# Context modulation after the first products instead of inside them, in a one-core hybrid attention and HGRN2 layer

## The chip, the cores and the metric

The kernel runs on one core of one Trainium2 chip. The number that counts is device time in microseconds (us) for one execution; three timed runs of the kernel before gave a median of 2031.61 us (2031.46 to 2032.01). Engines are named as in the profile: PE (TensorE matmul), PEld (its weight loads), DVE (VectorE), ACT (ScalarE), POOL (GpSimd) and SP (SyncE, whose queue here issues every DMA).

## What is computed

One layer takes 2048 latent tokens `x` and 256 context tokens `ctx`, all of width 1024. What matters for the change is its beginning:

```python
mod = silu(c) @ w_ada + b_ada            # for the latent tokens
shift, scale, gate = split(mod, 3)
mod_c = silu(c_ctx) @ w_ada + b_ada      # for the context tokens, same weights
shift_c, scale_c, _ = split(mod_c, 3)
h_lat = x * (1 + scale) + shift
h_ctx = ctx * (1 + scale_c) + shift_c
p_lat, p_ctx = h_lat @ w_in, h_ctx @ w_in   # 18 column units of 256
```

The columns of the products feed two mixers, a differential attention (`aq`, `ak`, `av`, gate `ag`) and a two-way gated scan (`ff`, `fb` forget gates, `hi` values, `hq` queries, gate `hg`). Of the context only `ak`, `av`, `ff`, `fb` and `hi` are needed. Then come the mixers, one output projection with `gate`, and a layer norm.

## The kernel before

**Products.** A unit is 256 columns of `w_in`. Every product is made of three matmuls on split operands: weights and tokens are each split into a rounded part and a rest (`wh`, `wl`; `hh`, `hl`), and `wl*hh`, `wh*hl`, `wh*hh` are added up in PSUM. `project_cols` (L507) makes 128x512 tiles, `project_tokens` (L526) 128x256 tiles for `hi` and `av`. Tokens come in four blocks of 512 (0 to 3) and the context block (number 4, of 256).

**Startup.** `startup()` makes the products of `ff0` and `ff1` on blocks 0 and 1 in four steps of two k rows each (L329, 48 matmuls a step, 192 in all), while the modulation that they need is still being made. A step loads four 512 KB rows of `w_ada` (tiles `wsh`, two of shift and two of scale), two `x` tiles (`xst`) and 256 KB of each unit's weights (`hh`, `hl` as raw tiles). Four dot products on DVE (`row_dot`, L392) turn rows of `w_ada` into columns of `mod`; ACT applies them to `x` (L444 and L445, both 128x512), and DVE makes the rests `hl` (L448) and `wl` (L457).

**Context modulation.** In the same steps `context_modulation` makes the context's columns of `mod` from the same `wsh` tiles: a multiplication on POOL (L403, 128x1024, two operands), a sum on ACT (L404) and a bias on POOL (L405), 16 times. Its row `silu(c_ctx)` is spread over the partitions by four small matmuls into `pa` (L385).

**After startup.** `project(HG_UNITS[2:], [0, 1, NBLK])` makes the pairs `fb`, `hi`, `hq` on blocks 0, 1 and the context. `merge` runs `gate_row` beside it, which loads the eight `wgate` rows, reduces them on DVE and stores `gate_d` in 4-byte elements. Then `project_rest` runs `ff` on the context and all `HG_UNITS` on blocks 2 and 3, now with the scan (`hgrn`) merged in at one scan step for three yields. A unit's weights are loaded into one raw buffer (`wraw`), then split into one of two sets (`wp[i % 2]`), which is free when the unit two places back has no product left. A tile of `ff` or `fb` is evacuated by ACT twice and DVE twice (L562 to L566) and stored to `FD` and `KD`; one of `hq` by ACT and DVE once and stored to `HQ`. The evacuation tiles (`e1`, `e2`) have two buffers, each free again when its store has landed; PSUM has four tiles (`pd`) for these products.

**What sets the order.** Each engine and the SP queue works in a fixed order, which the compiler's scheduler chose from the program text; a DMA behind one that waits, waits too.

## Time and profile before

| | before |
|---|---|
| median of 3 runs | 2031.61 us |
| the profiled execution | 2032.69 us |
| its span, first to last instruction | 2030.9 us |
| PE busy | 1913.6 us (94%) |
| DVE, ACT, POOL busy | 71%, 45%, 47% |
| DMA mean | 137 GB/s |

The span is what the rows below divide; 1.8 us of the profiled execution lie outside it. A busy PE says little by itself, since matmuls are pipelined: the distance between the starts of two matmuls tells more. 128x512 matmuls of this kernel start 0.227 us apart at their fastest. Shares over the whole span hide that the stages have different limits, so the rows below are taken from the first 300 us.

### The profile page before, as it was taken

The numbers are of one execution on the slowest core, as the hardware profiler recorded it, in microseconds if no ns is written. First come the engines' busy times: TensorE is split into PE (matmuls) and PEld (weight loads), VectorE is DVE, ScalarE is ACT, GpSimd is POOL, SyncE is SP. The second block draws the span as 40 slices with busy tenths as digits, with TensorE's granted clock in tenths as the row PEclk, the third lists the DMA queues.
The fourth block names the chain that finished last, engine by engine and source line by source line (L and its number), as shares of the span: only waits on it lengthen the run. The fifth ranks groups of instructions, "written<-read, shape, count | busy, mean of one in ns | idle before, by whom it ended". The sixth has DMA issues, their size and how long they took to land.

```text
span 2030.9 us, 32106 instructions
## 1 busy us (share of the span) xinstructions
PE 1913.6 (94%) x11716; PEld 1693.3 (83%) x11716; DVE 1438.3 (71%) x3022; ACT 920.4 (45%) x1383; POOL 955.6 (47%) x697
## 2 busy tenths in 40 slices
PE   5899999999989999999879999999999999998887
PEld 3689888998878898877667999999999999887676
DVE  8940475455676755678454279999999999967878
ACT  6731233222222222232100168999998889852211
POOL 6400063343554532535110047877877767755543
PEclk8999999999989999999889999999999999999999
DMA  5772564523344543353657652261261031145442
GB/s 221 248 221 81 186 220 164 182 99 125 113 136 150 167 151 138 110 169 102 199 169 229 199 148 59 68 169 54 62 169 57 28 102 37 51 136 173 154 139 92
DMA packets 177760, 278.05 MB, mean 137 GB/s; under 512 B 16577, under 2 KB 108993, under 8 KB 175554
## 3 DMA queue, kind: packets, MB, share of 16 engines
q1 hardware_dynamic: 177602, 276.00, 42.6%
q8 instruction: 93, 1.52, 0.3%
q14 instruction: 65, 0.53, 0.1%
HBM read 178.94 MB, written 97.00 MB: 136 GB/s over the span
## 4 chain that ended last, share of the span: by engine, by line
PE 66%; DVE 14%; DMA 10%; issue 4%; POOL 3%; ACT 2%; SPq 1%; DVEq 0%; POOLq 0%; ACTq 0%
PE pd L507 18%; PE po L1089 9%; PE pd L526 9%; PE s L1002 6%; PE s L1003 6%; PE pt L1069 6%; PE pl L723 4%; PE py L1301 2%; DVE wl L457 2%; DMA QLd<-e 1%; DMA KLd<-e 1%; PE pm L755 1%; DVE y L1305 1%; DVE wh L456 1%; DVE qq L731 1%
## 5 line engine op out<-in xcount | busy, mean ns | idle before, releaser
L1017 DVE TENSOR_SCALAR_CACHE_REDUCE e<-s 128x512 f32<-128x512 f32 (+1 forms) x512 | 372.8, 751 | 31.9 <-PE s L1003 31.5
L507 PE MATMUL pd<-hh,wl 128*128 128x512 f32 (+1 forms) x928 | 371.8, 401 | 0.0
L507 PE MATMUL pd<-hl,wh 128*128 128x512 f32 (+1 forms) x928 | 355.6, 383 | 0.0
L507 PE MATMUL pd<-hh,wh 128*128 128x512 f32 (+1 forms) x928 | 355.5, 383 | 0.0
L1052 POOL TENSOR_TENSOR e<-e,e 128x768 f32<-128x768 f32 (+1 forms) x192 | 351.5, 1860 | 2.6 <-ACT e L1045 0.2
L1026 ACT ACTIVATE e<-e,nm 128x2304 f32<-128x2304 f32 x128 | 286.5, 2238 | 1.7 <-DVE nm L1021 1.5
L728 POOL TENSOR_TENSOR kk<-kk,fb 128x512 f32<-128x512 f32 x126 | 170.5, 1353 | 169.7 <-DMA kk<-KD 136.5
L1002 PE MATMUL s<-kh,q 128*128 128x512 f32 (+1 forms) x640 | 244.3, 388 | 1.2 <-DVE w1l L1076 0.6
L1003 PE MATMUL s<-kl,q 128*128 128x512 f32 (+1 forms) x640 | 231.4, 371 | 0.0
L507 PEld LDWEIGHTS pd<-hh,wh 128*128 128x128 f32 x928 | 177.0, 191 | 34.3
L507 PEld LDWEIGHTS pd<-hh,wl 128*128 128x128 f32 x928 | 177.9, 192 | 27.6 <-DVE wl L457 0.5
L507 PEld LDWEIGHTS pd<-hl,wh 128*128 128x128 f32 x928 | 177.8, 192 | 27.1
L718 ACT COPY km<-kk 128x512 f32<-128x512 f32 x112 | 71.0, 635 | 271.6 <-POOL kk L728 179.9
L1047 POOL TENSOR_SCALAR e<-e,cf 128x1280 f32<-128x1280 f32 x64 | 86.2, 1346 | 175.3 <-DVE cf L1037 121.3
L1069 PE MATMUL pt<-eye,e 128*128 128x128 f32 x1152 | 162.8, 272 | 2.4 <-DVE rs L1268 0.9
L734 POOL TENSOR_TENSOR fb<-fb 128x512 f32<-128x512 f32 (+6 forms) x126 | 88.3, 701 | 162.4 <-DVE qq L731 152.3
L526 PE MATMUL pd<-wh,hl 128*128 128x256 f32 x512 | 150.8, 295 | 4.1 <-ACT wh L456 4.1
L723 PE MATMUL pl<-qq,km 128*128 128x128 f32 x896 | 131.3, 291 | 24.7 <-DVE qq L731 23.0
L723 PEld LDWEIGHTS pl<-qq,km 128*128 128x128 f32 x896 | 122.9, 197 | 37.1 <-issue 25.4
L1069 PEld LDWEIGHTS pt<-eye,e 128*128 128x128 f32 x1152 | 135.7, 140 | 21.2 <-issue 2.8
L526 PE MATMUL pd<-wl,hh 128*128 128x256 f32 x512 | 146.9, 287 | 0.1
L526 PE MATMUL pd<-wh,hh 128*128 128x256 f32 x512 | 146.7, 287 | 0.0
(286 smaller groups left out, 4463.7 us busy)
## 6 DMA issues: line engine op xcount, KB each, us to landing
wraw<-win SPq DMA_DIRECT2D x68, 512.0 KB
xst<-xT SPq DMA_DIRECT2D x24, 512.0 KB
fb<-FD SPq DMA_DIRECT2D x18, 512.0 KB
kk<-KD SPq DMA_DIRECT2D x18, 512.0 KB
kh<-KHd SPq DMA_DIRECT2D x16, 576.0 KB
FD<-e SPq DMA_DIRECT2D x32, 256.0 KB
KD<-e SPq DMA_DIRECT2D x32, 256.0 KB
Gd<-e SPq DMA_DIRECT2D x32, 256.0 KB
```

The source lines that it names most:

```text
L507: nc.tensor.matmul(ps[:, 0:n], a[:, k, cs], r[:, k, :], start=(k == 0 and j == 0), stop=(k == KT - 1 and j == 2))
L526: nc.tensor.matmul(ps[:, t, :], a[:, k, ts], r[:, k, :], start=(t == 0 and k == 0 and j == 0), stop=(t == 1 and k == KT - 1 and j == 2))
L723: nc.tensor.matmul(pl[:, e, ch, :], km[:, e, ch * P:ch * P + P], qm, start=True, stop=True)
L728: nc.gpsimd.tensor_tensor(out=o, in0=o, in1=total(fb, 1, 0, c), op=ALU.mult)
L734: nc.gpsimd.tensor_tensor(out=o, in0=o, in1=x, op=ALU.mult)
L1002: nc.tensor.matmul(ps[:, c:c + w], q[:, m, :], kh[m][:, a + c:a + c + w], start=True, stop=False)
L1003: nc.tensor.matmul(ps[:, c:c + w], q[:, 2 + m, :], kl[:, a + c:a + c + w], start=False, stop=True)
L1017: self.nc.vector.tensor_scalar(out=d[e][:, a:b], in0=d.pop(("s", m, i)), scalar1=1.0, scalar2=None, op0=ALU.mult, op1=ALU.max, accum_out=s ...
L1026: self.nc.scalar.activation(out=e, in_=e, func=AF.Exp, bias=self.tiles[t]["nm%d" % m], scale=1.0, accum_out=self.small(t, "z%d" % m))
L1052: self.nc.gpsimd.tensor_tensor(out=d["e0"][:, a:b], in0=d["e0"][:, a:b], in1=d["e1"][:, a:b], op=ALU.add)
L1069: self.nc.tensor.transpose(out=ps[:, k - a, :], in_=d["e0"][:, k * P:k * P + P], identity=self.b.eye)
L1089: nc.tensor.matmul(out, a[:, k - _GROUPS[g][0], :], w[:, :, k - _GROUPS[g][0], :], start=(op == self.value_ends[0] and k == k0 and j == 0) ...
```

## The change

`startup` no longer makes the context's columns of `mod`. A new side generator, `later_rows`, replaces `gate_row`: after startup it loads the 16 shift and scale rows of `w_ada` a second time, makes the context's columns from them by `row_dot` on DVE, prepares the context block (`prep_block(NBLK)`), and then does the eight `wgate` rows. It is merged at one step for five yields instead of twenty. The units are put in a new order, `ff`, `hq`, `fb`, `hi`, so that the pair right after startup needs no context. `wsh` has 11 buffers instead of 9, the second `xst` pool 2 instead of 1; the `junk` tile goes. `lower_bounds` is made in the second step instead of the first. The row for the context is loaded by a broadcast DMA, not spread by matmuls.

```diff
--- before.py
+++ after.py
@@ -44,7 +44,7 @@
 UW = 256
 
 UNITS = ["ak0", "ak1", "aq0", "aq1", "av0", "av1", "ag0", "ag1", "hg0", "hg1",
-         "ff0", "ff1", "fb0", "fb1", "hi0", "hi1", "hq0", "hq1"]
+         "ff0", "ff1", "hq0", "hq1", "fb0", "fb1", "hi0", "hi1"]
 GROUP_OF = {"aq": 0, "ak": 1, "av": 2, "ag": 3, "hq": 4, "hi": 5, "ff": 6, "fb": 7, "hg": 8}
 CTX_KINDS = ("ak", "av", "ff", "fb", "hi")
 ATT_UNITS = UNITS[:10]
@@ -244,7 +244,7 @@
             with ExitStack() as start:
                 self.ada = self.pool(start, "ada", 2)
                 self.startup()
-                for _ in self.merge(self.project(HG_UNITS[2:], [0, 1, NBLK]), self.gate_row(), 20):
+                for _ in self.merge(self.project(HG_UNITS[2:], [0, 1, NBLK]), self.later_rows(), 5):
                     pass
             rest = self.project_rest(att)
             with ExitStack() as scan:
@@ -280,9 +280,8 @@
 
 
         nc = self.nc
-        with ExitStack() as st:
-            rows = [self.silu_row(), self.silu_row_spread(self.pool(st, "pa", 2, space=PSUM))]
         self.constants()
+        self.row = self.silu_row(0, "row0")
         pair = HG_UNITS[:2]
         raw, split = [], []
         for i, u in enumerate(pair):
@@ -292,26 +291,24 @@
         with ExitStack() as st:
             pb = self.pool(st, "pb", 4, space=PSUM)
             acc = [[self.acc() for _ in range(4)], [pb.tile([P, BLK], F32, name="pb") for _ in range(4)]]
-            pending = []
             for k0 in range(0, KT, 2):
                 ks = slice(k0, k0 + 2)
                 w = []
                 for k in range(k0, k0 + 2):
                     for nm, src in ((0, "wshift"), (8, "wscale")):
-                        t = self.ada.tile([P, D], F32, name="wsh", bufs=9)
+                        t = self.ada.tile([P, D], F32, name="wsh", bufs=11)
                         self.load(t, self.I[src][k])
                         w.append((nm + k, t))
                 xs = []
                 for b in range(2):
-                    x = (self.wx if b == 0 else self.ada).tile([P, 1024], F32, name="xst", bufs=2 - b)
+                    x = (self.wx if b == 0 else self.ada).tile([P, 1024], F32, name="xst", bufs=2)
                     xs.append(x.rearrange("p (k n) -> p k n", n=BLK))
                     self.load(xs[b], self.I["xT"][b][:, ks, :])
                     if b == 0:
                         for i, u in enumerate(pair):
                             self.load(raw[i][:, ks, :], self.I["win"][UNITS.index(u)][:, ks, :])
                 for i, t in w:
-                    self.row_dot(self.mod[:, i, 0:1], t, rows[0], self.bias1[:, i:i + 1], junk=True)
-                pending.append(w)
+                    self.row_dot(self.mod[:, i, 0:1], t, self.row, self.bias1[:, i:i + 1])
                 self.modulate(0, k0, k0 + 1, xs[0], start=True)
                 for i in range(2):
                     self.split_unit(raw[i], split[i], k0, nc.scalar.copy, nc.vector)
@@ -333,11 +330,8 @@
                     if last and b == 1:
                         self.planned += 1
                         self.prefetch(i + 2)
-                if k0 == 0:
+                if k0 == 2:
                     self.lower_bounds()
-                while len(pending) > (1 if not last else 0):
-                    self.context_modulation(pending.pop(0), rows[1])
-            self.rows = rows
             self.late_constants()
 
     def project_rest(self, att):
@@ -359,59 +353,36 @@
         yield from self.project(LAST_UNITS[4:-1], [0, 1])
         self.held = self.project(LAST_UNITS[-1:], [1, 0])
 
-    def silu_row(self):
-
-        r = self.ada.tile([P, D], F32, name="row0", bufs=1)
-        self.load(r, self.I["cc"][0:1].partition_broadcast(P))
-        self.silu(r, self.ada.tile([P, D], F32, name="junk", bufs=1), self.nc.vector)
+    def silu_row(self, i, name):
+
+        nc = self.nc
+        r = self.ada.tile([P, D], F32, name=name, bufs=1)
+        self.load(r, self.I["cc"][i:i + 1].partition_broadcast(P))
+        sg = self.ada.tile([P, D], F32, name="wsh", bufs=11)
+        nc.scalar.activation(out=sg, in_=r, func=AF.Sigmoid)
+        nc.vector.tensor_tensor(out=r, in0=r, in1=sg, op=ALU.mult)
         return r
 
-    def silu(self, r, sg, eng):
-        self.nc.scalar.activation(out=sg, in_=r, func=AF.Sigmoid)
-        eng.tensor_tensor(out=r, in0=r, in1=sg, op=ALU.mult)
-
-    def silu_row_spread(self, pa):
-
-        nc = self.nc
-        one = self.ada.tile([P, D], F32, name="wsh", bufs=9)[:1]
-        ones = self.ada.tile([P, D], F32, name="wsh", bufs=9)[:1, :P]
-        self.load(one, self.I["cc"][1:2])
-        nc.gpsimd.memset(ones, 1.0)
-        self.silu(one, self.ada.tile([P, D], F32, name="wsh", bufs=9)[:1], nc.gpsimd)
-        r = self.ada.tile([P, D], F32, name="row1", bufs=1)
-        for half in range(2):
-            hs = slice(half * BLK, half * BLK + BLK)
-            ps = pa.tile([P, BLK], F32, name="pa")
-            nc.tensor.matmul(ps, ones, one[:, hs], start=True, stop=True)
-            nc.scalar.copy(out=r[:, hs], in_=ps)
-        return r
-
-    def row_dot(self, out, w, row, bias, junk=False):
-
-        dst = self.ada.tile([P, D], F32, name="junk", bufs=1) if junk else w
-        self.nc.vector.tensor_tensor_reduce(out=dst, in0=w, in1=row, scale=1.0, scalar=bias, op0=ALU.mult,
+    def row_dot(self, out, w, row, bias):
+
+        self.nc.vector.tensor_tensor_reduce(out=w, in0=w, in1=row, scale=1.0, scalar=bias, op0=ALU.mult,
                                             op1=ALU.add, accum_out=out)
 
-    def context_modulation(self, w, row):
-
-        nc = self.nc
-        for j, (i, t) in enumerate(w):
-            out, bias = self.mod[:, i, 1:2], self.bias1[:, i:i + 1]
-            if False:
-                self.row_dot(out, t, row, bias)
-            else:
-                nc.gpsimd.tensor_tensor(out=t, in0=t, in1=row, op=ALU.mult)
-                nc.scalar.activation(out=t, in_=t, func=AF.Copy, accum_out=out)
-                nc.gpsimd.tensor_tensor(out=out, in0=out, in1=bias, op=ALU.add)
-
-    def gate_row(self):
-        for _ in range(3):
+    def later_rows(self):
+
+        row = self.silu_row(1, "row1")
+        todo = [(nm + k, src, k) for k in range(KT) for nm, src in ((0, "wshift"), (8, "wscale"))]
+        for i, src, k in todo:
+            w = self.ada.tile([P, D], F32, name="wsh", bufs=11)
+            self.load(w, self.I[src][k])
             yield
+            self.row_dot(self.mod[:, i, 1:2], w, row, self.bias1[:, i:i + 1])
+        self.prep_block(NBLK)
         for j in range(KT):
-            w = self.ada.tile([P, D], F32, name="wsh", bufs=9)
+            w = self.ada.tile([P, D], F32, name="wsh", bufs=11)
             self.load(w, self.I["wgate"][j])
-            self.row_dot(self.gcol[:, j:j + 1], w, self.rows[0], self.bada[:, 16 + j:17 + j])
             yield
+            self.row_dot(self.gcol[:, j:j + 1], w, self.row, self.bada[:, 16 + j:17 + j])
         self.store(self.gate_d.rearrange("o (j p) -> p (o j)", p=P), self.gcol)
 
     def load_rope(self, half):
```

How the engines' orders move, at three places. Names with a number are buffers: `e_...` evacuation tiles, `row_...` the two silu rows.

POOL, from the first instruction to the scan, before:

```order
L371 TENSOR_TENSOR wsh<-wsh 1x1024
L403 TENSOR_TENSOR wsh<-wsh,row_221 128x1024 x3
L405 TENSOR_TENSOR mod<-mod,bias_235 128x1
L403 TENSOR_TENSOR wsh<-wsh,row_221 128x1024 x3
L405 TENSOR_TENSOR mod<-mod,bias_235 128x1
```

and now (`Sf`, `Sb` are the scan's states):

```order
L173 MEMSET eps 128x1
L598 MEMSET Sf_2052 128x256
L598 MEMSET Sb_2054 128x256
L598 MEMSET Sf_2056 128x256
L598 MEMSET Sb_2058 128x256
```

The 16 pairs of L403 and L405, of which the first rows stand above, are gone; POOL has no arithmetic before the scan.

SP, where the products of the first pair after startup are stored (`fb` before, `hq` now), before:

```order
L125 DMA wraw<-win 128x1024
L128 DMA FD_0_76<-e_800 128x512
L128 DMA KD_0_86<-e_801 128x512
L128 DMA FD_0_76<-e_833 128x512
L128 DMA KD_0_86<-e_834 128x512
L125 DMA wraw<-win 128x1024
L128 DMA FD_0_81<-e_866 128x512
L128 DMA KD_0_91<-e_867 128x512
```

and now:

```order
L125 DMA wsh<-wscale 128x1024
L128 DMA HQ_0_96<-e_726 128x512
L125 DMA wsh<-wshift 128x1024
L128 DMA HQ_0_96<-e_762 128x512
L125 DMA wsh<-wscale 128x1024
L128 DMA HQ_0_100<-e_795 128x512
L125 DMA wsh<-wshift 128x1024
L125 DMA wsh<-wscale 128x1024
L128 DMA HQ_0_100<-e_831 128x512
L125 DMA wsh<-wshift 128x1024
```

One store of a product stands between one to three loads of 512 KB, where there were two stores a product and few loads.

SP, around the store of `gate_d`, before (`FD_1_82` is block 1 of `fb1`, `FD_4_80` the context of `fb0`):

```order
L128 DMA FD_1_82<-e_998 128x512
L128 DMA KD_1_92<-e_999 128x512
L128 DMA gate_d<-gcol 128x8x1
L128 DMA FD_1_82<-e_1031 128x512
L128 DMA KD_1_92<-e_1032 128x512
L128 DMA FD_4_80<-e_1094 128x256
L128 DMA KD_4_90<-e_1095 128x256
```

and now (`FD_1_77` is block 1 of `fb0`):

```order
L128 DMA FD_1_77<-e_1210 128x512
L128 DMA KD_1_87<-e_1211 128x512
L128 DMA gate_d<-gcol 128x8x1
L125 DMA wraw<-win 128x1024
L125 DMA xst<-xT 128x1024
L128 DMA FD_1_77<-e_1249 128x512
L128 DMA KD_1_87<-e_1250 128x512
L125 DMA xst<-xT 128x1024
L125 DMA hq<-HQ_0_96 128x2x256
```

The small-element store now stands three tiles of `fb` further from the context's evacuations.

## Rows read from the trace of the kernel before

**Rows 1.** Waits of PE, 0 to 170 us: us in total, times, longest.
```profile
PE pd L329 <- DVE wl L457: 9.4, 3, 6.9
PE pd L329 <- DVE hl L448: 6.3, 2, 3.3
PE pd L526 <- ACT wh L456: 4.1, 1, 4.1
```
**Rows 2.** Busy time of each engine (instructions), granted clock, DMA share, GB/s, by stretch.
```profile
13.10:87.00 73.90, 54.50 (x193) 40.89 (x194) 71.46 (x73) 50.22 (x83) 53.06 (x31) 0.91 0.57 212
87.00:142.00 55.00, 55.00 (x289) 47.45 (x287) 29.86 (x65) 25.23 (x47) 2.18 (x6) 1.00 0.89 257
147.00:155.00 8.00, 8.00 (x45) 8.00 (x46) 4.22 (x9) 3.03 (x8) 0.00 (x0) 0.63 0.66 211
155.00:207.00 52.00, 52.00 (x435) 52.00 (x435) 3.79 (x6) 8.40 (x15) 0.00 (x0) 1.00 0.22 74
```
**Rows 3.** Groups by line, 0 to 170 us: busy, mean ns, idle before, releaser.
```profile
L403 POOL TENSOR_TENSOR wsh<-wsh,row 128x1024 f32<-128x1024 f32 x16 | 43.0, 2693 | 16.4 <-DVE mod L392 9.1 <-ACT row L386 5.3 <-DVE lbmx L200 1.8
L392 DVE CUSTOM_DVE_ANT_0 junk<-wsh,row,bias 128x1024 f32<-128x1024 f32 x16 | 33.5, 2092 | 0.2
L448 DVE TENSOR_TENSOR hl<-xst,hh 128x512 fp32r<-128x512 f32 (+1 forms) x24 | 22.8, 958 | 0.3 <-ACT xst L445 0.2
...
L444 ACT ACTIVATE hh<-xst,mod 128x512 fp32r<-128x512 f32 x16 | 12.5, 807 | 18.0 <-DVE mod L392 18.0
...
L457 DVE TENSOR_TENSOR wl<-hl,wh 128x512 fp32r<-128x512 f32 x4 | 9.3, 2334 | 0.0
```
**Rows 4.** DVE in order of time, third step of startup: start, us, instruction.
```profile
43.31 0.68 DVE L448 TENSOR_TENSOR hl<-xst,hh 128x512 fp32r<-128x512 f32 x1
43.91 1.27 DVE L392 CUSTOM_DVE_ANT_0 junk<-wsh,row,bias 128x1024 f32<-128x1024 f32 x1
...
45.72 3.40 DVE L392 CUSTOM_DVE_ANT_0 junk<-wsh,row,bias 128x1024 f32<-128x1024 f32 x1
```
**Rows 5.** POOL in order of time, at the same place.
```profile
45.27 2.77 POOL L403 TENSOR_TENSOR wsh<-wsh,row 128x1024 f32<-128x1024 f32 x1 [3.04 <-DVE mod L392]
```
**Rows 6.** PE in order of time, start and end of startup.
```profile
13.16 1.22 PE L329 MATMUL pd<-hh,wl 128*128 128x512 f32 x2 [0.15 <-ACT hh L444]
...
19.16 0.63 PE L329 MATMUL pd<-hl,wh 128*128 128x512 f32 x1
...
19.59 0.63 PE L329 MATMUL pd<-hh,wh 128*128 128x512 f32 x1
...
86.95 0.39 PE L507 MATMUL pd<-hh,wl 128*128 128x512 f32 x1
```
**Rows 7.** In order of time, SP, ACT and PE from `fb` to `hi`.
```profile
130.90 0.38 SPq L128 DMA_DIRECT2D gate_d<-gcol  x1
...
141.50 0.38 ACT L562 ACTIVATE e<-pd 128x256 f32<-128x256 f32 x1 [6.18 <-DMA FD<-e]
...
145.61 2.17 ACT L456 CAST wh<-wraw 128x512 fp32r<-128x512 f32 x4
...
146.28 0.58 PE L526 MATMUL pd<-wh,hl 128*128 128x256 f32 x1 [4.14 <-ACT wh L456]
```
**Rows 8.** As Rows 2: what the DMA engines moved in single stretches.
```profile
6.00:10.00 4.00, 0.77 (x1) 0.50 (x2) 2.35 (x3) 1.28 (x2) 2.43 (x1) 1.00 1.01 394
...
105.00:110.00 5.00, 5.00 (x24) 4.14 (x23) 1.34 (x3) 1.64 (x3) 0.00 (x0) 1.00 1.06 270
...
125.00:130.00 5.00, 5.00 (x23) 4.13 (x22) 3.86 (x7) 1.09 (x2) 0.00 (x0) 1.00 1.03 371
...
135.00:140.00 5.00, 5.00 (x44) 5.00 (x43) 0.84 (x2) 0.32 (x1) 0.00 (x0) 1.00 0.85 55
```
**Rows 9.** In order of time, SP and DVE: the weights of `ff1` for its second pass.
```profile
247.09 0.80 SPq L125 DMA_DIRECT2D wraw<-win  x2
...
250.92 0.76 DVE L456 CAST wh<-wraw 128x512 fp32r<-128x512 f32 x2 [1.48 <-PE pd L507]
```

## The prediction

> **What bounds the kernel now.** I read the table of stages first. PE is busy 94% of the span, so only a stage in which it is held up can give time back. The first 87 us are such a stage: DVE is busy 71.46 of 73.9 us there, PE is not [rows 2]. The 192 matmuls of startup would take 192 x 0.227 = 43.5 us at the distance that the profile shows at its fastest; they begin at 13.16 and the next product begins at 86.95 [rows 6], so 73.8 us go by. PE's waits name the operands that DVE makes, `wl` and `hl` [rows 1]. Some matmuls also start 0.43 us apart (19.16, 19.59 [rows 6]) after such a gap.
>
> Why DVE is full is read from its groups. A row dot takes 1.27 us and an `hl` 0.68 us when nothing is beside them [rows 4], but the 16 row dots average 2.09 us and the four late `wl` 2.33 us [rows 3]. In order of time the slow ones lie beside POOL: a row dot that begins at 45.72 ends at 49.12 [rows 4], while POOL's L403 runs from 45.27 to 48.04 [rows 5]: it ends 1.08 us after POOL did, about its own length. So DVE stands still while POOL works and then runs. ACT waits for DVE in turn, 18.0 us for `mod` [rows 3].
>
> The next place where PE stands is the passage from `fb` to `hi`: 4.14 us before the first matmul of `hi` [rows 7], then slow matmuls: 45 of them in 8 us, where the stretch behind has 435 in 52 [rows 2].
>
> **Startup.** The change takes the 16 L403 (43.0 us on POOL [rows 3]), the 16 sums on ACT and the four small matmuls out of the stage. DVE gives back, by the means against the undisturbed lengths, 16 x (2.09 - 1.27) = 13.1 us of row dots, about 22.8 - 16 x 0.68 - 8 x 0.42 = 8.6 us of `hl` (8 of the 24 are halves, at an estimated 0.42), 4 x (2.33 - 0.68) = 6.6 us of `wl`: 28 us, and more in the small operations of `lower_bounds`. What is left for DVE in a step is 4 row dots, 4 `hl`, 2 `wl`: 4 x 1.27 + 6 x 0.68 = 9.2 us. For ACT it is 8 operations of 0.81 [rows 3] and 2 casts of 2.17 / 4 = 0.54 us [rows 7], 7.6 us. PE needs 48 x 0.227 = 10.9 us. So PE becomes the longest of the three, and the stage should end when PE has done its work: first useful matmuls at about 14 us (13.16 now, for the same first row dots), 43.5 us of matmuls, and 24 of them at the slow distance at the start, 24 x 0.2 = 4.8 us: 62.3 us in place of 86.95, a gain of 24.6 us. The bounds: at best 12 slow matmuls and no wait, 13.2 + 43.5 + 2.4 = 59 us, a gain of 28; at worst DVE and ACT don't overlap, 9.7 + 4 x 16.8 + 5.4 (the last half step of PE) = 82 us, a gain of 5. I take the first, since ACT and DVE work on different blocks in the order shown and overlap already. The loads don't hold it: 15.4 MB in the stage at 394 GB/s [rows 8] are 39 us, and the last `x` tile is wanted at about 52.
>
> The Trainium skill, "SBUF — State Buffer", section "Who interferes with whom", says that a DVE instruction with two inputs in SBUF and a GpSimd instruction that reads SBUF exclude one another for the whole instruction. The rows agree for this pair. By the page each of the 16 L403 could block DVE for its mean of 2.69 us, 43 us at most, against the 28 that the means show. Neither would alter the end of startup, which PE sets by then.
>
> **The second reading of w_ada.** It adds 16 loads of 512 KB, a row of 512 KB, 16 row dots and one more silu to the stage behind. DVE does 24 x 1.27 = 30.5 us of row dots there instead of 10.2; it is busy only 29.9 of 55 us [rows 2], and PE has four PSUM tiles of 5.4 us (24 x 0.227) before a late evacuation stops it, so I cost them at nothing; without that cover 20 us would be lost. The evacuations of `hq` stand on DVE behind row dots that wait for a load, but these loads are issued a tile earlier. On SP, between two stores of `hq`, there are one to three loads, at most 1.57 + 0.26 MB in 5.4 us. From the first load after startup to the context's stores of `fb` the queue moves 39 x 0.524 + 43 x 0.262 + 1.1 = 32.8 MB, against 18.9 in the same stretch before. This stretch runs, as I reckon, from 47 us to 62.3 + 2 x 43.5 = 149 us (`hq` and `fb` on two blocks), 102 us. Loads at 394 GB/s and stores at 270 [rows 8] make 21.7 / 0.394 + 11.1 / 0.270 = 96 us. It fits, barely; I take 0 and bound it by the slower rival below. The context's columns are wanted at 149 us, 90 us after startup, and the row dots end near 115.
>
> **From fb to hi.** ACT's evacuation of the context tile waits 6.18 us for an `FD` store; ACT then casts `hi`'s weights, and PE waits for these [rows 7]. The stores were late because `gate_d` in 4-byte elements had been issued at 130.90 [rows 7]: from 135 to 140 the DMA engines are 0.85 busy with 55 GB/s [rows 8]. Now this store stands three tiles, some 16 us, further ahead. The wait should go: 4.1 us, and the slow matmuls behind it, 8 - 45 x 52 / 435 = 2.6 us, 6.7 us in all. Bounds 0 (the queue is still full) and 6.7; I take 6.7, because nothing of size is issued after the sixth tile of `fb`.
>
> **From hi to ff.** `hi` is now last, so between the last use of one weight set and its next stands a context tile of 24 x 2 short matmuls (0.12 each, 5.7 us) instead of a block of 10.9 us. The weights of `ff1` come by a load issued when `ff0`'s have been split (247.09 before) and split by DVE from 250.92 [rows 9], with 4 more modulations of block 3 in between. Load, these, and the split together end some 13 us after the release; PE comes there after 11.4 and eats k rows as they come. Bounds 0 and 5, I take 1. Behind the last unit PE's order is the same in both kernels, so all of this shifts what follows and nothing else.
>
> **The sum.** 2032.7 (the profiled execution) - 24.6 - 6.7 + 1 = 2002.4 us. The median of the runs is 1.1 lower, so 2001.3; I say 2002.
>
> **Rivals.** *ACT paces startup.* ACT's second `hh` of a step stands behind the step's fourth row dot, and all its other work behind that. If half of ACT's 7.6 us is on the path, a step takes 13.0: 9.7 + 52 + 5.4 = 67 us, a gain of 19.8; with the stall at `hi` kept it ends at 2032.7 - 19.8 + 1 - 1.1 = 2013. For it: ACT's 18 us of waits for `mod` [rows 3]. Against it: most of that wait was DVE's.
> *Everything fits better.* Startup ends at 59 and nothing is lost later: 2032.7 - 28 - 6.7 - 1.1 = 1997.
> *DMA becomes the bound, and the kernel gets slower.* The stretch from 47 to 149 us has 32.8 MB. At the 257 GB/s that 87 to 142 us showed [rows 2] it takes 128 us and ends 25 us late. The loads of `hi`'s weights are at its end, so PE would wait there for all of it, and be slow behind it: 2032.7 - 24.6 + 25 + 2.6 + 1 - 1.1 = 2036. It decides below 32.8 / (102 + 24.6) = 259 GB/s. For it: stores alone ran at 270 [rows 8]. Against it: 371 in a stretch of mostly loads [rows 8], and those 257 at 0.89 busy were what was asked for.
> *The change doesn't free startup.* If it were the loads that pace it, at the 212 GB/s of now [rows 2] 15.4 MB take 73 us and little is won, about 2030. The rows speak against it: DVE, not DMA, is what PE waits for.
>
> **How the numbers follow.** The forecast (1997 to 2008) 0.57, ACT paces 0.20, better than 1997 0.10, a part of the DMA case (2015 to 2027) 0.05, no gain 0.03, slower 0.05. The likeliest is the forecast: 2002. The range, 1994 to 2018, leaves out the ends. A measurement of this kernel tells about 0.2%, 4 us, from no change. Faster takes in all but the last two: 0.92; same 0.03; slower 0.05.
>
> **What would show it.** Right: the first matmul of `hq` near 62 us; row dots of 1.3 us and `hl` of 0.7 in startup; no wait of PE for casts between `fb` and `hi`; DMA busy near 1 from 60 to 130 us; behind the first scan groups the same waits as before, some 30 us earlier. Wrong: PE waiting for `hl` at each step with DVE idle (ACT paces); PE waiting for `wraw` or ACT for a store from 100 to 160 us (DMA paces); matmuls 0.43 us apart through all of startup.

## The result, and the profile after

| | before | after |
|---|---|---|
| median of 4 runs each, same chip | 2031.53 us (2028.42 to 2032.01) | 2009.74 us (2004.60 to 2011.88) |
| the profiled execution, its span | 2032.69, 2030.9 | 2008.39, 2006.6 |
| DVE, ACT, POOL busy | 71%, 45%, 47% | 71%, 45%, 45% |
| HBM read, DMA mean | 178.94 MB, 137 GB/s | 187.85 MB, 143 GB/s |

The ratio is 0.9892 with an interval of 0.9870 to 0.9914: 22 us faster. The forecast was 2002 us in a range of 1994 to 2018, so the time lies inside it, 7.7 us above the forecast and 1.7 above the narrower stretch (1997 to 2008) that the prediction called the forecast.

Startup first. These are PE's rows around its end in the kernel after (start, us), the busy time of the engines by stretch as in [rows 2], two groups of DVE in startup (busy us, mean ns), and PE's waits from 0 to 300 us (us in total, times, longest):

```profile
60.46 0.39 PE L326 MATMUL pb<-hh,wh 128*128 128x512 f32 x1
60.68 0.39 PE L478 MATMUL pd<-hh,wl 128*128 128x512 f32 x1
```

```profile
13.00:60.60 47.60, 46.18 (x192) 36.92 (x193) 38.04 (x75) 36.48 (x56) 0.00 (x0) 1.00 0.85 322
60.70:105.00 44.30, 44.30 (x197) 36.70 (x196) 32.08 (x58) 15.88 (x29) 0.00 (x0) 1.00 0.94 311
105.00:149.00 44.00, 44.00 (x201) 36.63 (x200) 26.12 (x49) 10.68 (x21) 1.62 (x4) 1.00 0.92 261
```

```profile
L368 DVE CUSTOM_DVE_ANT_0 wsh<-wsh,row,bias 128x1024 f32<-128x1024 f32 x16 | 20.1, 1280 | 0.0
...
L419 DVE TENSOR_TENSOR hl<-xst,hh 128x512 fp32r<-128x512 f32 x16 | 10.9, 690 | 8.2 <-ACT xst L416 8.2
```

```profile
PE pd L326 <- ACT hh L415: 13.1, 1, 13.1
PE pd L478 <- ACT e L534: 3.2, 2, 1.7
PE pd L497 <- ACT wh L427: 1.1, 1, 1.1
PE pd L326 <- DVE wl L428: 1.0, 1, 1.0
PE pd L326 <- DVE hl L419: 0.4, 1, 0.4
PE pd L497 <- DVE wl L428: 0.3, 1, 0.3
```

The first matmul of `hq` starts at 60.68 where the next product started at 86.95 [rows 6]. The 13.1 us are the wait for the first operand. After it PE waits 1.4 us in all of startup, against the long waits for `hl` and `wl` of [rows 1]. DVE is busy 38.04 of 47.6 us and no longer 71.46 of 73.9 [rows 2]; a row dot takes 1280 ns, not 2092 [rows 3]. From 60.7 to 149 us, with the second reading of `w_ada` in it, PE does not stop, at a DMA share of 0.92 to 0.94.

Then comes the passage from `fb` to `hi`, where the four other waits of the list lie. SP, ACT and PE there in order of time, kernel after (start, us; in brackets the idle time ahead and what ended it), and two stretches between:

```profile
138.22 0.38 SPq L128 DMA_DIRECT2D gate_d<-gcol  x1
138.65 0.57 SPq L125 DMA_DIRECT2D wraw<-win  x1
139.27 0.42 SPq L125 DMA_DIRECT2D xst<-xT  x1
139.79 0.38 SPq L128 DMA_DIRECT2D FD<-e  x1
140.26 0.41 SPq L128 DMA_DIRECT2D KD<-e  x1
140.76 0.51 SPq L125 DMA_DIRECT2D xst<-xT  x1
```

```profile
137.54 0.60 ACT L534 ACTIVATE e<-pd 128x512 f32<-128x512 f32 x1
152.75 1.52 ACT L416 ACTIVATE xst<-xst,mod 128x512 f32<-128x512 f32 x2 [14.62 <-DMA xst<-xT]
154.18 0.57 ACT L533 ACTIVATE e<-pd 128x512 f32<-128x512 f32 x1
```

```profile
155.29 0.39 PE L478 MATMUL pd<-hh,wl 128*128 128x256 f32 x1 [1.66 <-ACT e L534]
...
160.00 0.39 PE L478 MATMUL pd<-hh,wl 128*128 128x256 f32 x1 [1.57 <-ACT e L534]
...
164.26 0.38 PE L497 MATMUL pd<-wh,hl 128*128 128x256 f32 x1 [1.12 <-ACT wh L427]
```

```profile
140.00:145.00 5.00, 5.00 (x23) 4.13 (x22) 0.00 (x0) 0.00 (x0) 0.00 (x0) 1.00 1.17 91
145.00:150.00 5.00, 5.00 (x33) 4.53 (x32) 0.00 (x0) 0.00 (x0) 0.00 (x0) 1.00 0.73 63
```

The stall is still there. Right behind the 4 KB of `gate_d` stand a load of weights (`wraw`) and the tokens of block 2 (`xst`). For ten microseconds the DMA engines are busy (shares of 1.17 and 0.73) and move 91 and 63 GB/s, the first `x` tile lands 13 us after its issue, and ACT waits 14.62 us for it with the evacuations of `fb` queued behind. PE has its four PSUM tiles as cover and loses 4.7 us. `hi` begins at 164.26; without waits it would be 60.68 + 87 + 11.4 = 159.1.

To see where the rest went I compare when the same matmul starts in both traces, counted from the last one (PE's order is the same behind the last unit). The **lead** of the kernel after is 26.3 us at the end of startup, 28.1 at 260 us, 29.5 at 980, 26.7 from 1110 to 1700, 24.7 just behind 1760, 24.3 at the end (the difference of the two spans). So 26.3 + 1.8 are won by 260 us, and 3.8 us are given back much later: in the last backward scans (about 980 to 1110 us) and within 5 us near 1760. (Times of this paragraph are the kernel before's.)

### The profile page after: what moved, and what is told of

It reads as the page before. It is cut to its first block, busy times and chain, and to the rows that moved or that the text cites. A ratio compares the mean times of both kernels' runs of the same rounds, so it can differ in the third digit from the quotient of the medians.

```text
span 2006.6 us, 32053 instructions
## 1 busy us (share of the span) xinstructions
PE 1901.3 (95%) x11712; PEld 1686.6 (84%) x11712; DVE 1426.1 (71%) x3055; ACT 903.4 (45%) x1349; POOL 894.1 (45%) x663
## 3 DMA queue, kind: packets, MB, share of 16 engines
HBM read 187.85 MB, written 97.00 MB: 142 GB/s over the span
## 4 chain that ended last, share of the span: by engine, by line
PE 63%; DVE 14%; DMA 12%; issue 4%; ACT 3%; POOL 3%; SPq 1%; DVEq 0%; POOLq 0%; ACTq 0%
PE pd L478 16%; PE po L1060 9%; PE pd L497 8%; PE s L973 6%; PE s L974 6%; PE pt L1040 6%; PE pl L694 4%; DMA QLd<-e 2%; PE py L1272 2%; DVE wl L428 2%; DMA KLd<-e 1%; DVE wsh L368 1%; PE pm L726 1%; DMA wraw<-win 1%; DMA kh<-Od 1%
## 5 line engine op out<-in xcount | busy, mean ns | idle before, releaser
L988 DVE TENSOR_SCALAR_CACHE_REDUCE e<-s 128x512 f32<-128x512 f32 (+1 forms) x512 | 372.8, 751 | 31.7 <-PE s L974 31.2
L705 POOL TENSOR_TENSOR fb<-fb 128x512 f32<-128x512 f32 (+4 forms) x126 | 83.2, 661 | 162.5 <-DVE qq L702 148.0
```

Source lines behind the costliest of these rows:

```text
L988: self.nc.vector.tensor_scalar(out=d[e][:, a:b], in0=d.pop(("s", m, i)), scalar1=1.0, scalar2=None, op0=ALU.mult, op1=ALU.max, accum_out=s ...
```

## The experiments

Theory G: the store of `gate_d`, 1024 elements of 4 bytes, holds the DMA engines for about 10 us, and whoever waits for a transfer then waits as long. Theory S: the second reading has filled the queue. Theory L: in startup GpSimd stops DVE. Theory P came up on the way. Each group of runs shared its own runs of the kernel before, so the ratios are what compare; leads are of one profile each. Of the variants of the kernel after (`a_...`) only `a_gate_rows` and `a_rows_pool51` have an interval clear of its own; what the others show of the stall, they show in their traces.

| kernel | median us | ratio to before, interval | lead at 260 | 1700 | 1760 | end |
|---|---|---|---|---|---|---|
| after | 2009.74 | 0.9892 (0.9870 to 0.9914) | 28.1 | 26.7 | 24.7 | 24.3 |
| a_gate_late | 2005.24 | 0.9880 (0.9863 to 0.9897) | 31.7 | 35.4 | 31.8 | 29.2 |
| a_gate_rows | 2000.94 | 0.9854 (0.9839 to 0.9869) | 33.4 | 33.3 | 29.7 | 30.4 |
| a_gate_after_hi | 2002.85 | 0.9871 (0.9857 to 0.9886) | 33.8 | 33.9 | 30.3 | 30.0 |
| a_gate_twice | 2010.49 | 0.9915 (0.9900 to 0.9930) | 26.0 | 21.5 | 17.9 | 18.1 |
| a_one_reading | 2002.85 | 0.9864 (0.9848 to 0.9880) | 33.4 | 31.5 | 29.5 | 29.2 |
| a_rows_pool51 | 1998.00 | 0.9848 (0.9830 to 0.9866) | 32.8 | 31.9 | 31.9 | 32.6 |
| b_gate_late | 2029.98 | 0.9996 (0.9986 to 1.0007) | 3.8 | 4.4 | 4.5 | 5.2 |
| b_gate_rows | 2026.20 | 0.9991 (0.9982 to 0.9999) | 6.3 | 7.5 | 7.5 | 7.9 |
| b_new_order | 2028.70 | 0.9990 (0.9977 to 1.0003) | 7.0 | 6.1 | 4.0 | 1.8 |
| b_no_context | 2009.79 | 0.9897 (0.9880 to 0.9913) | 27.5 | 27.8 | 24.2 | 23.1 |
| b_ctx_on_dve | 2014.53 | 0.9923 (0.9906 to 0.9940) | 20.9 | 23.0 | 21.0 | 18.2 |
| b_pool77 | 2035.23 | 1.0019 (1.0006 to 1.0032) | 0.4 | 1.0 | -2.6 | -3.8 |

### The store of gate_d

```diff
+        for _ in range(20):
+            yield
         self.store(self.gate_d.rearrange("o (j p) -> p (o j)", p=P), self.gcol)
```

The same in the kernel before, with 5 in place of 20, is `b_gate_late`.

> The changed kernel with only the store of gate_d issued later: twenty steps of the merge (some 68 us) behind the last row dot, in the middle of hi, where the DMA engines are 0.2 to 0.5 busy. Theory G (the 1024 four-byte elements of gate_d hold the DMA engines for some 10 us, 140 to 150 us in the changed kernel: share 1.17 at 91 GB/s, then 0.73 at 63): block 2's x tiles land within 6 us of their issue, ACT's wait of 14.6 us before the modulation falls below 4, PE's 4.7 us of waits between fb and hi fall below 1.5, and the median falls by some 4 us, from 2009.7 to about 2005.5. Theory S (the second reading of w_ada has filled the queue, and the stores and loads stand behind it): ACT still waits over 10 us, PE over 3.5, and the time stays at 2009 to 2010.

> The kernel before with only the store of gate_d issued later: five steps of its merge (some 68 us) behind the last row dot. Theory G: ACT's wait of 6.2 us for an FD store and PE's 4.1 us at hi go, and with them the slow matmuls behind (2.6 us): some 4 to 6.5 us off the 2031.5, about 2026. Rival (the stores of fb simply stand in a full queue, gate_d or not): PE still waits 3 to 4 us and the time stays within 2 us of 2031.5.

Neither told anything on G, because the edit did not do what it says. The store has nothing to wait for but `gcol`, and the scheduler put it where `gcol` is ready: 139.15 us in place of 138.22, and 130.06 in place of 130.90. In `a_gate_late` ACT still waits 12.6 us for `x`. PE's waits came out at 1.1 us there and the median at 2005.24, both as G had it, and neither counts, since the store had not moved. What the two kernels did show is how much such a passage varies: with the store in the same place in the kernel before, and with only a load of weights now ahead of it in `a_gate_late`, the lead at 260 us came out 3.8 and 3.6 us larger. A difference of that size in a single profile decides nothing here.

```diff
-        self.store(self.gate_d.rearrange("o (j p) -> p (o j)", p=P), self.gcol)
...
+        ps = self.acc()
+        nc.tensor.transpose(out=ps[0:KT, 0:P], in_=self.gcol, identity=self.eye)
+        g = self.ada.tile([P, P], F32, name="grow", bufs=1)[0:KT, :]
+        nc.scalar.copy(out=g, in_=ps[0:KT, 0:P])
+        self.store(self.gate_d.rearrange("o (j p) -> (o j) p", p=P), g)
```

> The changed kernel with gate_d stored from rows: two merge steps (about 7 us) after the last row dot the 128x8 tile is transposed by one matmul, copied by ACT and stored as 8 rows of 512 bytes in place of 1024 elements of 4 bytes. Theory G (the small elements are what costs): as with the late store, ACT's wait below 4 us, PE's below 1.5, about 2005.5 us. If any store at this place stands behind a full queue, or the wait comes from the second reading (theory S): ACT's wait stays over 10 us and the time at 2009 to 2010.

The stretches and ACT's wait in this kernel:

```profile
140.00:145.00 5.00, 5.00 (x24) 4.14 (x23) 1.22 (x2) 0.42 (x1) 0.55 (x3) 1.00 0.96 338
145.00:150.00 5.00, 5.00 (x32) 4.46 (x31) 1.93 (x4) 4.45 (x8) 0.00 (x0) 1.00 0.32 122
150.00:155.00 5.00, 5.00 (x45) 4.98 (x44) 0.80 (x3) 1.41 (x4) 0.00 (x0) 1.00 0.60 173
155.00:160.00 5.00, 5.00 (x44) 5.00 (x43) 3.82 (x8) 3.01 (x7) 0.00 (x0) 1.00 0.75 233
```

```profile
ACT xst L423 <- DMA xst<-xT: 6.1, 1, 6.1
```

With no store of `gate_d` ahead, the engines move 338 GB/s from 140 to 145 us, and PE has no wait at all between 60 and 300 us. ACT's wait is 6.1 us and not below 4 as expected; the lead is 33.4. The transposed store left SP at 151.15, behind the two `x` loads. In the ten microseconds behind it the engines move 173 and 233 GB/s at shares of 0.60 and 0.75: nothing like the 63 GB/s at 0.73 above. But since the store has moved too, this run does not tell whether its form or its place took the wait away. The next one shows what the place does.

```diff
...
+                late = self.const.tile([P, KT], F32, name="late")
+                self.load(late, self.HV[0][1][:, 0, 0:KT])
+                nc.gpsimd.tensor_copy(out=late, in_=self.gcol)
+                self.store(self.gate_d.rearrange("o (j p) -> p (o j)", p=P), late)
```

(The store in `later_rows` goes.)

> The changed kernel with the store of gate_d really moved: it goes through a copy on GpSimd that first waits for a small load of hi's own output, so that it can be issued only some 25 to 35 us into hi. (Written later but with nothing to wait for, it had stood in nearly the same place on SP's queue: 139.15 instead of 138.22 us.) Theory G: the passage from fb to hi is as with the rows store: ACT's wait for x near 6 us, PE's waits below 1, the lead over the kernel before at 260 us is 33 instead of 28 us, the time 2000 to 2003; the 4-byte elements cost nothing in the middle of hi, where nothing is waited for. Theory S: as the changed kernel, 2009.

As G has it. The store of 4-byte elements went out at 196.23 and slowed the engines there just the same, but nobody was waiting: no wait of PE, lead 33.8.

```profile
195.00:200.00 5.00, 5.00 (x44) 5.00 (x44) 0.00 (x0) 2.67 (x4) 0.19 (x1) 1.00 0.68 164
200.00:205.00 5.00, 5.00 (x44) 5.00 (x43) 0.00 (x0) 0.84 (x2) 0.00 (x0) 1.00 0.65 49
```

> The changed kernel with the cost in dispute doubled: directly behind the store of gate_d the same 1024 four-byte elements are stored once more, into a scratch row that nobody reads. Theory G (these elements hold the DMA engines some 10 us): ACT's wait for block 2's x grows from 14.6 to 20 to 25 us, PE's waits between fb and hi from 4.7 to 10 to 15, and the median rises from 2009.7 to 2015 to 2019. Theory S alone (a full queue from the second reading, 4 KB more don't matter): within 2 us of 2009.7.

The direction in the trace is right and the size is not. The two stretches fell to 67 and 23 GB/s, ACT waited 17.8 us instead of 14.6, PE 4.9 us in one piece with a granted clock of 0.76 and 0.56 behind it, and the lead at 260 us fell by 2.1 us, not by 5 to 10. A second thousand elements cost 3 us more on ACT in this profile, not another ten: the cost is not in proportion to the number of elements. The median, 2010.49, lies where theory S alone had it, and the ratio's interval overlaps that of the kernel after, so the time of this run decides nothing between G and S. In the DMA records the 4-byte packets themselves are through within 2 us (3 with the store doubled); it is the 4 KB packets that start 4 to 9 us behind the issue that take 1.2 to 2.3 us each, at most 3.0 (1.8 to 3.3, at most 4.7, with the store doubled), where most took 0.16 before. Why those slow down, no run here shows.

```diff
             yield
-            self.row_dot(self.mod[:, i, 1:2], w, row, self.bias1[:, i:i + 1])
+        self.nc.vector.tensor_copy(out=self.mod[:, :, 1:2], in_=self.mod[:, :, 0:1])
```

> The changed kernel without the second reading: the 16 loads of w_shift and w_scale, their row dots and the second silu are left out of the stage behind startup, and the context columns of the modulation are copied from those of the other tokens (the context is then modulated by the wrong row); the merge steps, the loads of w_gate and the store of gate_d stay where they were. The prediction costs the second reading at nothing. Theory G: the passage from fb to hi keeps ACT's wait of 10 to 15 us and PE's of about 4.7, and the time is 2009.7 within 2 us. Theory S: both waits go, and the time falls by 4 to 5 us, to about 2005.

(The loads in front of the `yield` go too.) By what I wrote down, S has won: no wait, lead 33.4. But look at where `gate_d` went. Without the 16 rows ahead of it in `later_rows` it was issued at 97.22, while `hq` ran, and there too the engines fell to 18 GB/s, with PE never waiting:

```profile
97.22 0.43 SPq L128 DMA_DIRECT2D gate_d<-gcol  x1
```

```profile
100.00:105.00 5.00, 5.00 (x24) 4.14 (x23) 0.69 (x1) 2.53 (x5) 0.00 (x0) 1.00 0.69 18
```

And `a_gate_rows` and `a_gate_after_hi` have the second reading, and leads of 33.4 and 33.8. So the second reading costs nothing by its bytes; by these profiles it cost 5.3 us (33.4 - 28.1) by pushing the store from 97 to 138 us, into a passage that can't bear it.

> The kernel before with only the store of gate_d as 8 rows of 512 bytes (transposed by one matmul, copied by ACT). Theory G: the 4.1 us that PE waits at hi and the slow matmuls behind go, 5 to 6.5 us: 2024.5 to 2026 against 2030.8. Rival (in the kernel before, the FD stores stand in a full queue anyway): PE still waits 2 us or more there, and the time is within 2 us of 2030.8.

The wait at `hi` is gone (no wait of PE from 100 to 300 us) and the lead is 6.3, as G has it. Here the rows left only at 245.26 us, so the edit moved the store as well. By the ratio the gain is only 0.1%, 2 us (interval 0.2 to 3.7), not the 5 to 6.5 expected. Perhaps the other executions of the kernel before did not all have the whole stall of the profiled one: `b_gate_late`, with the store in the same place, has 2.3 us of waits there and not 4.1. No profile of those executions shows it.

### The order of the units, and startup

```diff
-         "ff0", "ff1", "fb0", "fb1", "hi0", "hi1", "hq0", "hq1"]
+         "ff0", "ff1", "hq0", "hq1", "fb0", "fb1", "hi0", "hi1"]
```

> The kernel before with the units in the new order alone (hq ahead of fb and hi). Startup is as before and ends near 87 us; the store of gate_d is issued near 130 us, beside hq, and hi comes 43 us later. Theory G: nothing waits for a transfer where the store is issued, so that PE's 4.1 us of waits and the slow matmuls between fb and hi go, and hi to ff1 costs nothing: 5 to 6.5 us less, 2023.5 to 2025 where the kernel before has 2028.5 to 2031. Rival (the passage from fb to hi waits because two units' stores, hi's weights and block 2's x come together there, whatever the store of gate_d does): PE waits 3 us or more there, within 2 us of the kernel before.

The store left at 125.30, beside `hq`, the engines fell to 57 and 71 GB/s, and PE did not wait at any point from 88 to 300 us, the passage from `hi` to `ff1` included: lead 7.0. In this trace the order does what the prediction said of it, as long as nothing delays the store. In the time it is not seen: the ratio, 0.9990, can't be told from 1, where 5 to 6.5 us were expected. Of the 5.2 us that the lead loses up to the end, 2.1 are told below; the others are open.

```diff
-                    self.context_modulation(pending.pop(0), rows[1])
+                    pending.pop(0)
...
+            nc.vector.tensor_copy(out=self.mod[:, :, 1:2], in_=self.mod[:, :, 0:1])
```

> The kernel before without its context modulation in startup: the 16 multiplications of GpSimd, the 16 sums of ACT and the 16 small additions are left out, and the context columns are copied from those of the other tokens (the context is then modulated by the wrong row); the spread of the second silu row, the order of the units and everything behind stay. This is the startup part of the change alone. Theory L (GpSimd's work stops DVE for as long as it runs): row dots 1.3 us, hl 0.7, wl 0.7, startup ends near 62 us instead of 87, and the time falls by 22 to 26 us from 2030, to 2004 to 2008, the stall between fb and hi staying as it was; GpSimd's stream is shorter, which may cost 2 to 3.6 us at the end of the attention, as in the kernels with 51 fewer. Rival (the loads, or ACT's and PE's own order, pace startup): it ends at 73 us or later, and the time is 2017 or more.

Startup ends at 60.5, the row dots take 1.28 us: L, not the loads. The time falls by 21 us (ratio 0.9897), just short of the 22 to 26 expected and as much as the whole change won. The stall behind it is the old one, earlier: `gate_d` was issued at 104.60, and from 110 to 115 us the engines were busy (1.03) with 11 GB/s. ACT waited for an `FD` store:

```profile
118.54 0.38 ACT L563 ACTIVATE e<-pd 128x256 f32<-128x256 f32 x1 [10.00 <-DMA FD<-e]
```

That kernel reads `w_ada` once, so S is out for this stall.

```diff
-            if False:
+            if True:
                 self.row_dot(out, t, row, bias)
```

> The kernel before with the context columns of startup made by DVE: 16 more row dots there in place of 16 multiplications and 16 additions on GpSimd and 16 sums on ACT; same loads, same result. DVE, which is full, gets 16 x 1.3 = 20 us more work. Theory L (what DVE loses is the time in which GpSimd holds SBUF): without GpSimd beside it DVE needs 4 x (9.2 + 5.2) = 57 us in the four steps, startup ends at 72 to 75 us instead of 87, and the time falls by 10 to 15 us to 2016 to 2021 although DVE does more. Rival (DVE is simply full of its own work): startup ends at 100 us or later, and the time is 2043 or more.

The plainest test of L: DVE gets 16 row dots more, and startup ends 24 us earlier, at 62.80; the ratio is 0.9923, 16 us. DVE is full, and PE hardly waits; the second row shows the added row dots (ns least/median/most, first and last start):

```profile
13.00:62.00 49.00, 46.79 (x189) 37.26 (x190) 48.96 (x93) 34.73 (x53) 0.00 (x0) 1.00 0.88 312
```

```profile
L392 DVE CUSTOM_DVE_ANT_0 wsh<-wsh,row,bias x16: 1278/1283/1293, 16.0 to 69.8; 128x1024 f32<-128x1024 f32 x16
```

I had expected 72 to 75, from 57 us of DVE's work begun at 13 us. But three of the added dots fall behind the end of startup, up to 71 us, where no product needs them yet, and the first row dots and a `wl` are done before 13 us; 49 us of work are left. This edit and the one of `b_no_context` also take the 16 sums off ACT, so neither run alone tells GpSimd from ACT. The trace of the kernel before does. All 13 row dots, `hl` and `wl` of its startup that took 2.8 us or more overlap a multiplication of GpSimd by at least 2.3 us, and row dots that ran beside ACT's sums alone kept their length:

```profile
25.83 1.04 ACT L404 ACTIVATE wsh<-wsh 128x1024 f32<-128x1024 f32 x1
26.20 1.28 DVE L392 CUSTOM_DVE_ANT_0 junk<-wsh,row,bias 128x1024 f32<-128x1024 f32 x1
```

In `b_ctx_on_dve` the passage to `hi` has the old stall once more (PE waits 4.0 us for ACT, 1.4 for the weights), with `gate_d` issued at 104.77 and 24 GB/s from 110 to 115 us; hence 20.9 at 260.

### The end of the attention

Near 1760 us the kernel after and each of its variants but `a_rows_pool51` lost 2 to 3.6 us of their lead within 5 us, and `b_gate_late` and `b_gate_rows` lost none (the column 1760 of the table is read just behind, at 1765). POOL and DVE there, first in the kernel before (rows not shown so far), then in the kernel after:

```profile
1752.92 0.21 DVE L1037 SCALAR_TENSOR_TENSOR cf<-cf,z,neglam 128x1 f32<-128x1 f32 x1
...
1754.75 0.47 DVE L1279 CAST kl<-kh 128x512 fp32r<-128x512 f32 x1
```

```profile
1753.59 1.35 POOL L1047 TENSOR_SCALAR e<-e,cf 128x1280 f32<-128x1280 f32 x1 [2.58 <-DVE cf L1037]
1754.89 3.27 POOL L1052 TENSOR_TENSOR e<-e,e 128x512 f32<-128x512 f32 x2
```

```profile
1726.23 0.21 DVE L1008 SCALAR_TENSOR_TENSOR cf<-cf,z,neglam 128x1 f32<-128x1 f32 x1
...
1728.06 1.42 DVE L1250 CAST kl<-kh 128x512 fp32r<-128x512 f32 x1
```

```profile
1726.61 1.34 POOL L1018 TENSOR_SCALAR e<-e,cf 128x1280 f32<-128x1280 f32 x1 [2.28 <-DVE cf L1008]
1727.91 3.28 POOL L1023 TENSOR_TENSOR e<-e,e 128x512 f32<-128x512 f32 x2
```

In the kernel before POOL begins 0.46 us behind `cf`'s end, and DVE's cast starts 0.14 us ahead of POOL's addition: 0.47 us. In the kernel after POOL begins after 0.17 us, its addition is 0.15 us ahead of the cast, and the cast takes 1.42. Then PE waits 2.5 us for `w0l` and `w3l`, and 0.8 in the kernel before. The instructions on both engines are the same there; what differs is that POOL's stream has 51 fewer ahead (914 recorded instead of 965; 1049 and 1100 in all). Theory P: the place in the stream decides.

```diff
+            pad = self.ada.tile([P, 1], F32, name="pad", bufs=1)
+            for _ in range(51):
+                nc.gpsimd.memset(pad, 0.0)
```

> The kernel with the rows store of gate_d, and 51 one-element memsets on GpSimd in startup, where that engine is idle, so that each later GpSimd instruction has the same place in its stream as in the kernel before (1100 recorded instead of 1049). In both kernels in the old count GpSimd starts one multiplication near the end of the attention 0.46 us behind its operand and DVE's two casts of kl beside it take 0.47 us; in the four kernels with 51 fewer it starts after 0.17 and the casts take 1.42 to 1.55, PE waits 1.8 us more and the lead falls by 2 to 3.6 us there. Theory P (the place in the instruction stream sets that delay, and the delay sets who holds SBUF first): delay 0.46, casts 0.47, and 2 to 3.6 us less than with the rows store alone, 1997.3 to 1999. Rival (it follows from the earlier start of the kernel, or from the other data's timing): delay 0.17, casts 1.4 to 1.55, 2001.

> The kernel before with 77 one-element copies on GpSimd behind the store of gate_d, at 130 to 140 us, where that engine is idle, so that every later GpSimd instruction stands 77 places further back. Theory P (the place in GpSimd's stream sets whether it starts 0.46 or 0.17 us behind its operand near the end of the attention): the delay of 0.46 us leaves that place, DVE's two casts of kl take 1.4 to 1.55 us instead of 0.47, and the time rises by 2 to 3.6 us over the kernel before. Rival (the casts' length hangs on something else that the change of startup altered): casts 0.47 us and no change.

The two casts in four kernels, `a_gate_rows`, `a_rows_pool51`, before, `b_pool77` (ns least/median/most, first and last start):

```profile
L1257 DVE CAST kl<-kh x2: 1431/1492/1552, 1721.4 to 1726.9; 128x512 fp32r<-128x512 f32 x2
```

```profile
L1260 DVE CAST kl<-kh x2: 452/471/490, 1722.9 to 1727.3; 128x512 fp32r<-128x512 f32 x2
```

```profile
L1279 DVE CAST kl<-kh x2: 465/478/490, 1754.8 to 1759.2; 128x512 fp32r<-128x512 f32 x2
```

```profile
L1282 DVE CAST kl<-kh x2: 1428/1487/1546, 1753.7 to 1759.2; 128x512 fp32r<-128x512 f32 x2
```

P holds both ways: 51 idle memsets give the short casts back and the lead stays at 31.9 through 1760; 77 idle copies take them from the kernel before, and it gets slower (1.0019, interval above 1). `b_new_order`, with one recorded POOL instruction fewer in all (963 ahead of this place), has casts of 1.43 us already and loses 2.1 us here, `b_no_context` and `b_ctx_on_dve` 3.6 and 2.0. In all 14 profiles the start is 0.46 us behind `cf` where 965 instructions stand ahead (four profiles) and 0.17 where another number does (914 to 919, 963, 1042). Over the 13 profiles compared with the one of before the lead falls by 2 us or more near 1760 where the casts are long, and by nothing where they are short. Between `a_gate_rows` and `a_rows_pool51` the time does not show it: the ratios are 0.9854 and 0.9848, with intervals that overlap.

`a_rows_pool51` has the lowest ratio, clear of the kernel after, but not of `a_gate_rows` or `a_one_reading`.

## Why the prediction was right, and where it was not

**Startup** (62.3 us predicted, 60.68 measured; 24.6 us, measured 26.3). Right in mechanism and nearly in size. The matmuls at the slow distance were dearer in the sum than in fact: by the means of the three `pd` groups (437, 410, 404 ns against 389, 32 each) they cost 2.7 us, not 4.8. With the start at 13.1 and 1.4 us of waits that gives 60.7. What GpSimd took from DVE was put at 28 us from the means; DVE's 71.46 us of [rows 2] became 38.04 for much the same work, 33 us. By the rule of the Trainium skill ("SBUF — State Buffer", "Who interferes with whom") the 16 multiplications, 43.0 us [rows 3], could block DVE for that long at most, an estimate, and the trace agrees.

**The rival "ACT paces startup"** gave 2013, closer to 2009.7 than the forecast on paper and wrong in fact: ACT was busy 36.48 of 47.6 us and PE waited 0.0 us for it after the first operand. A number near the result is no evidence for its story. The range reaches to 2018 for this rival's sake; that it also holds the 3.8 us lost late in the kernel, for which the sum had no term, is luck.

**The second reading at nothing.** Right for its bytes (264 GB/s from 47 to 149 us were enough, PE did not stop). One reading under it was wrong: the 270 GB/s of [rows 8] are not of stores alone, as a load of 512 KB (`wraw`) is issued at 105.90, beside three stores of 256 KB. The step that was missing: the reading stands ahead of the gate rows in the same generator, so it delays all that follows them there. I had costed the loads and not the order behind them.

**From `fb` to `hi`** (6.7 us predicted). This is the step that failed: 1.8 us came. PE's waits did not go, they are 4.7 us instead of 4.1. What went are the slow matmuls (2.6 us): the granted clock is 1.00 (2.4 GHz) from 149 to 173 us, with PE's waits in four pieces of at most 1.7 us, where it was 0.63 on average from 147 to 155 us [rows 2], behind one wait of 4.1. The prediction named the cause, `gate_d`, and said the store would be far enough ahead, "because nothing of size is issued after the sixth tile of `fb`". In fact a `wraw` load, two `x` loads, `FD`, `KD` and three `hq` loads stand directly behind it, as the order of SP that was written down ahead of the prediction already lists (up to the first `hq`), and ACT's fixed order puts block 2's modulation ahead of the evacuations. I had looked for who waits for a store, as in [rows 7], and not for who waits for a load. With the store in rows or really moved the lead grows by 7.7 and 7.6 us from the end of startup to 260 us (25.7 to 33.4, 26.2 to 33.8), near the 6.7 predicted; whether the form of the store or its place matters in the first of these, the runs leave open.

**From `hi` to `ff`** (1 us predicted): 0; no wait of PE in any kernel with the new order.

**"All of this shifts what follows and nothing else"** did not hold: 3.8 us went. About 2 of them are theory P. The others, from 980 to 1110 us, are open: PE waits there for the states of the backward scan, 15.1 us in three waits for `Sb` in the profile after, 11.5 before and 12.3 in `a_gate_rows`, and from profile to profile the lead moves there by -3.8 to +3.4 us.

The sum by the traces: 2032.7 - 26.3 - 1.8 + 3.8 = 2008.4, the profiled execution.

## What to carry to other kernels

When work is moved behind something in a generator or a queue, cost what it delays, not only what it adds: the second reading was free, and the small store that it pushed 40 us back cost 5 in the profile. A store in 4-byte elements belongs where nobody waits for a load or a store in the next 10 us, or is turned into rows first; and after an edit that is meant to move an instruction, read in the trace whether it moved. Two profiles that differ by 3 us far from the edit deserve a look at which engine began first there.

## What was not expected of the hardware

In each of the eleven profiles in which it ran, a 4 KB store in 1024 elements was followed within 11 us by a stretch of 5 us in which the DMA engines moved 11 to 94 GB/s at a share of 0.65 to 1.13; ahead of it they had moved 247 to 388 GB/s (162 in `a_gate_after_hi`). Eight rows of 512 bytes left no such mark (173 and 233 GB/s at shares of 0.60 and 0.75 in `a_gate_rows`). The Trainium skill ("DMA: Bandwidth & Descriptors", "Specifications") puts the least size of a transfer for full rate at 512 bytes and says that smaller ones are read, changed and written back. The traces agree at the two sizes that ran: the rate falls behind elements of 4 bytes and not behind rows of 512. What lies between, and whether that writing back is the reason, no run here shows. That the later, large packets are what slows down, and that twice the elements made ACT wait 17.8 us instead of 14.6 and no more, was new.

A cast with one input in SBUF is held by GpSimd as well: 0.47 us when it starts 0.14 us ahead of GpSimd's addition, 1.42 us when it starts 0.15 us behind. The Trainium skill ("SBUF — State Buffer", "Who interferes with whom") says that copies and casts can, under its conditions, take both ports and that whoever comes first keeps them for its whole instruction; the trace agrees: the long cast ends 0.28 us behind the end of the addition that was ahead of it.

51 idle instructions more on GpSimd in one kernel, or 77 in another, 1600 us earlier, move one start there by 0.29 us (0.46 against 0.17 behind the operand) and so change who comes first. By what the place in the stream acts was not found.
